# One input of a two-layer diffusion backbone loaded through another engine's queue, and one tile's low part made by another engine

## The chip, the cores and the metric

The kernel runs on one core of a Trainium2 chip. The metric is the time of one execution on the device, in microseconds. Five engines with their own instruction streams share the work: TensorE (PE, matrix products; PEld are its weight loads), VectorE (DVE), ScalarE (ACT), GpSimd (POOL) and SyncE (SP). They meet only through semaphores. Sixteen DMA engines move data between the chip's DRAM and its on-chip memory; here SP and ACT issue the transfers, each in its own instruction stream. A transfer that stands between two computations of ACT is issued when ACT gets there, and what stands behind it waits for it to be issued.

## The reference, cut to what matters

```python
for i in range(2):
    h_lat = rms_norm(x_lat, norm_g[i]) * (1 + sc_l) + sh_l      # 1024 latent tokens, width 1024
    h_ctx = rms_norm(x_ctx, norm_g[i]) * (1 + sc_c) + sh_c      # 256 context tokens
    if i % 2 == 0:   # two groups of 8 heads: A global attention, B windowed attention with a sink
        q, k, v, gate = split(h @ w_in)
        y = concat(A(q, k, v) * silu(gate), B(q, k, v) * silu(gate)) @ w_out
    else:            # convolution module and neighbourhood attention
        y = concat(conv(h), D(h) * silu(gate)) @ w_out
    x_lat = x_lat + g_l * y_lat                                 # the layer's input is added again
    x_ctx = x_ctx + g_c * y_ctx
return rms_norm(x_lat, final_g)
```

All of it is single precision. The two lines that matter here are the attention's product with the values, softmax(q k) v, and the residual sum, which needs the layer's input x a second time, after the attention.

## The kernel before

**Numbers in two parts.** TensorE is given each single-precision matrix as a high part (a rounded copy, made by ACT, line 336) and a low part (the number minus its rounded copy, made by POOL or DVE, line 339). `split` does this; its last argument names the engine of the low part, `"g"` for GpSimd and `"v"` for VectorE. A product is then three matmuls (lines 374 to 376).

**The first attention.** `attn_gen` goes through 252 items in the first layer. An item is a tile of 128 keys by 512 columns (128 queries of four heads). For each item PE makes the scores `st` (lines 543 and 547), ACT the exponential `pf` (line 555) and its high part `ph` (line 336), and POOL the low part `pl` (line 339); three items later PE multiplies `ph`, `ph` and `pl` with the values into `ov` (lines 483, 484 and 485). Every twelfth item (`vshare`, here 12) has its low part made by DVE instead. The scores have two PSUM banks, so PE can be at most two items ahead of ACT's exponentials. When a block of 128 queries is done, DVE transposes the sums (line 493), multiplies with the gate (713), inverts (496), spreads (497) and scales (717); the result `y` goes to DRAM (`Od`, line 720) or, for the last quarter of the heads, is split in place into `hh` and `hl`, a part of the input of the output projection.

**Woven into it.** While the last quarter of the heads is attended, the output projection of the first layer for the other three quarters runs between the attention's items (`out0_part`, products `po`, lines 374 to 376): for each pair of output columns `load_w` fetches six pieces of the weights (`wr<-ev_wo`, line 385), and at the first pass `load_x1` fetches the layer's input for these columns into `x1`, in three pieces: 256 context tokens (256 KB) and twice 512 latent tokens (512 KB each). Four calls make twelve transfers and 5 MB. DVE adds the products to `x1` in place (line 1198). The last quarter's own projection (`final_proj`) follows with and after the end of the attention; then `norm_h` and `make_h1` make the second layer's input (lines 354, 365, 366, 368 and 336/339).

**Order.** The kernel is written as generators that are interleaved by `weave`; a scheduler then orders each engine's instructions by priority and by its own estimate of time, and each engine runs its list strictly in that order. Every transfer gets one of eight completion semaphores, taken in turn by all transfers of both queues, and is not issued before the transfer that used the same semaphore last has landed. So at most eight transfers are under way, and a queue waits at its head for the one eight places back.

Of the kernel before, what the change touches and what calls it, by code (L numbers as in the profile page):

```python
# [101 lines left out]
def tile_kernel(ctx: ExitStack, tc: tile.TileContext, a, out):  # L102
    nc = tc.nc
    VE, SC, GP, PE, SY = nc.vector, nc.scalar, nc.gpsimd, nc.tensor, nc.sync
# [9 lines left out]
    mk, mwp, hold, layer, spare = [0], [None], [0], [0], []  # L114
# [3 lines left out]
    def bank(tag, name):  # L118
        if tag == "pp" and solo[0] and not sums[0]:
            turn[0] += 1  # L120
            tag = ("pp", "mx")[turn[0] // 2 % 2]
        return ps.tile([P, 512], F32, tag=tag, name=name, bufs=BUFS[tag])
# [3 lines left out]
    def nm(s):  # L126
        uid[0] += 1
        return f"{s}_{uid[0]}"
# [205 lines left out]
    def split(src, hi, lo, heng="s", leng="g"):  # L334
        if heng == "s":
            cast[0] = SC.copy(hi, src)  # L336
        else:
            VE.tensor_copy(hi, src)
        i_ = (GP if leng == "g" else VE).tensor_tensor(lo, src, hi.bitcast(F32), op=ALU.subtract)  # L339
        cast[2 if leng == "g" else 1] = i_  # L340
# [104 lines left out]
    def cut(ap, q, n):  # L445
        if isinstance(q, tuple):
            return ap.rearrange("p (r c) -> p r c", c=32)[:, q[0] : q[0] + q[1], q[2] : q[2] + q[3]]
        return ap[:, q : q + n]

    def flat(ap, q, n):  # L450
        return ap[:, :n].rearrange("p (r c) -> p r c", c=q[3]) if isinstance(q, tuple) else ap[:, :n]
# [12 lines left out]
    def attn_gen(pool, groups, vshare, look, nexts=None):  # L464

        preps = [g.prep for g in groups]
        items = [(g, t) for g in groups for t in range(len(g.tiles))]
        pend = []
        cnt = [0]

        def flush():
            g, t, ph, pl = pend.pop(0)
            k, q0, n, _ = g.tiles[t]
            if t == 0:
                g.ov = bank("mx" if g is groups[-1] and not layer[0] else "ov", nm("ov"))
                if g.load_v is not None:
                    g.load_v()
            V, vo = g.v(k)
            vo *= VW
            last = t == len(g.tiles) - 1  # L480
            o, ph, pl = cut(g.ov, q0, n), flat(ph, q0, n), flat(pl, q0, n)
            m = P if t == 0 else VW - 64
            PE.matmul(o[0:m], V[:, vo + 64 : vo + 64 + m], ph, start=(t == 0), stop=False)  # L483
            PE.matmul(cut(g.ov[0:64], q0, n), V[:, vo : vo + 64], ph, start=False, stop=False)  # L484
            pvs.append(PE.matmul(o[0 : VW - 64], V[:, vo + 64 : vo + VW], pl, start=False, stop=(last and g.sink is None)))  # L485
            if last:
                if g.sink is not None:
                    PE.matmul(g.ov, g.skm(), g.QL[0:76, :], start=False, stop=True)
                r1 = pool.tile([P, 8, 32], F32, tag="r1", name=nm("r1"), bufs=1)
                r8 = pool.tile([P, 8], F32, tag="r8", name=nm("r8"), bufs=2)  # L490
                rb = pool.tile([P, 256], F32, tag="rb", name=nm("rb"), bufs=1)
                for e in range(2):
                    VE.transpose(r1[e * 64 : (e + 1) * 64].rearrange("p a b -> p (a b)")
                                 .rearrange("p (a q) -> p a q", a=2), g.den(g.ov[64:128, :], e))
                yu = g.pre(g.ov)
                VE.reciprocal(r8, r1[:, :, 0])
                VE.transpose(rb, r8[:, :, None].broadcast_to([P, 8, 32]))
                g.finish(yu, rb)
# [13 lines left out]
        def prepare(x, n):  # L512

            while n and work and work[0][0] <= x:
                if next(work[0][1], work) is work:
                    work.pop(0)
                else:
                    n -= 1
# [7 lines left out]
        for x, (g, t) in enumerate(items):  # L526
            if x + AHEAD < len(items):
                items[x + AHEAD][0].ahead(items[x + AHEAD][1])
            if t == 0:
                g.start()  # L530
                while any(p is g.prep for _, p in work):
                    prepare(len(items), 1)
                for k in g.ids:
                    next(preps[k])
                    work.append((x + LEAD[layer[0]], preps[k]))
            rate = g.rate * max(len(work), 1)
            k, q0, n, extra = g.tiles[t]
            KA, KB = g.k()
            st = bank("st", nm("st"))
            kp = g.kpos[k] if g.bias else k  # L540
            cs = slice(kp * P, (kp + 1) * P)
            sf = flat(st, q0, n)
            sts.append(PE.matmul(sf, KA[:, cs], cut(g.QH, q0, n), start=True, stop=False))  # L543
            if not g.bias:
                for lhs, rhs in extra():
                    PE.matmul(st[:, :n], lhs, rhs, start=False, stop=False)
            PE.matmul(sf, KB[0:68, cs], cut(g.QL[0:68], q0, n), start=False, stop=True)  # L547
            ph = pool.tile([P, 512], F32R, tag="ph", name=nm("ph"), bufs=look + 1)
            pl = pool.tile([P, 512], F32R, tag="pl", name=nm("pl"), bufs=look + 1)
            pf = pool.tile([P, 512], F32, tag="pf" if layer[0] else "ost", name=nm("pf"), bufs=PFB)  # L550
            if g.bias and extra is not None:
                VE.tensor_tensor(flat(pf, q0, n), sf, extra(), op=ALU.add)
                SC.activation(pf[:, :n], pf[:, :n], AF.Exp)
            else:
                SC.activation(pf[:, :n], st[:, :n], AF.Exp, scale=1.0 if g.bias else SCALE)  # L555
            cnt[0] += 1
            split(pf[:, :n], ph[:, :n], pl[:, :n], "s", "v" if cnt[0] % vshare == 0 else "g")
            pend.append((g, t, ph, pl))
            tailc[:] = cast
            if t == len(g.tiles) // 2:  # L560
                g.gate()
            if t == len(g.tiles) - 1:
                g.last()
            prepare(x, rate // 2)
            yield
            if len(pend) > look:
                flush()
            prepare(x, rate - rate // 2)
            yield
# [166 lines left out]
    with ExitStack() as p0x:  # L736
# [307 lines left out]
        for j in PIECES:  # L1044
            load_kv(ORDER[0], *PIECES[j])
        SY.dma_start(KBs[ORDER[0]][0:64, :].bitcast(F32), Kd[ORDER[0]][0:64])
        main = attn_gen(a0, [group0(u, qb) for u in ORDER for qb in QORD], VS0, LOOK0)
        for k in range(3):
            u = ORDER[k]
            unit[0] = k  # L1050
            n = NSTEP[u // 2] + (12 if k == 0 else 0)
# [110 lines left out]
    with tc.tile_pool(name="o0", bufs=1, reuse_waits="tile", side="right") as op_:  # L1162
# [4 lines left out]
        x1 = []  # L1167
# [13 lines left out]
        def load_x1(e2):  # L1181
            for c in range(3):
                t0, n = CHUNKS[c]
                es = slice(2 * e2, 2 * e2 + 2)
                SC.dma_start(x1[c][:, es], a["cT"][:, es] if c == 0 else a["xT"][:, es, t0 - 256 : t0 - 256 + n])

        WO = 8

# [12 lines left out]
        def out0_part(fs):  # L1201
            for e2 in range(4):
                w = load_w(op_, a["ev_wo"], e2 * 256, 256, 256, WO, dks=fs, rb=2)
                if fs == parts[0]:
                    load_x1(e2)
                for e in (2 * e2, 2 * e2 + 1):
                    for c in range(3):
                        yield from out0(fs, e, c, *w)
# [83 lines left out]
    with ExitStack():  # L1292
# [476 lines left out]
        def ends(evs):  # L1769
            for ev in evs:  # L1770
# [8 lines left out]
                else:  # L1779
                    yield from final_norm(k, bcs[k])  # L1780

        main = attn_gen(dpool, groups1, VSH, LOOK1, {11: [], 12: [13, 14], 13: [15]})
        weave(main, WV[0], d_proj(2), 31, False, True, LAG[0])
        weave(main, WV[1], d_proj(3), 31, False, True, LAG[1])
# [149 lines left out]
```

## Time and profile before

| | us |
|---|---|
| median of three runs | 1478.57 (1475.46 to 1480.4) |
| the profiled execution, its own time | 1479.93 |
| its span | 1477.8 |
| PE busy in the span | 1415.7 (96%) |
| DVE, POOL and ACT busy | 1059.0, 828.4 and 741.1 |

The span reaches from the first to the last instruction; 2.1 us of the execution's time lie outside it. The stage that the change touches lies between 600 and 880 us of the span, counted from its start. In views of the timeline a row gives the start and the duration in microseconds, the engine (SPq and ACTq are issues of transfers), the line, the operation, the tiles, and in square brackets the idle time before it and what ended it.

### The profile page before, as it was taken

Reading aid. Unit: us, or ns where it says so; the run is one execution under the profiler, and the core shown is the slowest. Engines: PE = TensorE matmul, PEld = TensorE weight load, DVE = VectorE, ACT = ScalarE, POOL = GpSimd, SP = SyncE. Lnnn points to the kernel's source line nnn. Section 1 sums busy time; section 2 is a strip of 40 time slices with the busy share of each in tenths; the row PEclk is TensorE's granted clock in tenths of the full one; section 3 lists DMA queues with packets and bytes.
Section 4 is the critical chain, followed back from the end, with each engine's and each line's share of the span. In section 5 each row is a group of like instructions: output and inputs, shape, how many; then the busy total and the mean of one; then the engine's idle time right before and its main releaser. Section 6 shows DMA issues by size and latency. Waiting matters only on the chain.

```text
span 1477.8 us, 22207 instructions
## 1 busy us (share of the span) xinstructions
PE 1415.7 (96%) x7078; PEld 1151.4 (78%) x7078; DVE 1059.0 (72%) x2109; ACT 741.1 (50%) x1540; POOL 828.4 (56%) x819
## 2 busy tenths in 40 slices
PE   7899999999999999999999989999999999999996
PEld 2798978887888777667877778888887888778775
DVE  4786577589857786758666786999837575477775
ACT  3631453645364674764444655443434354555563
POOL 3561462656566785875554776754543343555564
PEclk9999999999999999999999999999999999999998
DMA  9675145323631235363222231213595877788623
GB/s 349 215 225 158 47 139 159 99 68 121 186 104 54 73 95 182 111 212 90 72 69 61 93 101 57 86 59 87 162 315 190 232 237 229 230 284 267 209 80 121
DMA packets 185228, 219.05 MB, mean 148 GB/s; under 512 B 17548, under 2 KB 136536, under 8 KB 185112
## 3 DMA queue, kind: packets, MB, share of 16 engines
q1 hardware_dynamic: 174864, 199.77, 43.3%
q10 hardware_dynamic: 10248, 17.87, 3.8%
q8 instruction: 56, 0.92, 0.3%
q14 instruction: 60, 0.49, 0.1%
HBM read 155.45 MB, written 62.13 MB: 147 GB/s over the span
## 4 chain that ended last, share of the span: by engine, by line
PE 79%; DVE 8%; DMA 7%; issue 2%; ACT 2%; POOL 1%; SPq 1%; ACTq 0%; DVEq 0%; POOLq 0%
PE p L374 7%; PE p L375 7%; PE p L376 7%; PE ov L483 4%; PE ov L485 4%; PE st L543 4%; PE ov L484 4%; PE st L547 4%; PE po L374 4%; PE po L375 4%; PE po L376 4%; PE pq L374 3%; PE pq L376 3%; PE pq L375 3%; PE pg L374 2%; PE pg L375 2%
## 5 line engine op out<-in xcount | busy, mean ns | idle before, releaser
L339 POOL TENSOR_TENSOR pl<-pf,ph 128x512 fp32r<-128x512 f32 (+1 forms) x327 | 385.9, 1193 | 242.4 <-ACT ph L336 190.2
L339 POOL TENSOR_TENSOR wl<-wr,wh 128x256 fp32r<-128x256 f32 (+2 forms) x253 | 193.2, 782 | 125.0 <-ACT wh L336 85.9
L555 ACT ACTIVATE pf<-st 128x512 f32<-128x512 f32 x284 | 166.1, 597 | 155.7 <-PE st L547 132.0
L336 ACT CAST ph<-pf 128x512 fp32r<-128x512 f32 (+3 forms) x364 | 203.3, 572 | 17.7 <-PE ov L484 6.7
L374 PE MATMUL p<-hh,wh 128*128 128x512 f32 x448 | 177.7, 399 | 1.1 <-ACT wh L336 1.0
L375 PE MATMUL p<-hl,wh 128*128 128x512 f32 x448 | 178.1, 400 | 0.0
L376 PE MATMUL p<-hh,wl 128*128 128x512 f32 x448 | 173.9, 397 | 0.2 <-POOL wl L339 0.2
L336 ACT CAST wh<-wr 128x256 fp32r<-128x256 f32 (+2 forms) x260 | 101.3, 404 | 140.5 <-DMA wr<-in_od_d_dram 38.6
L483 PE MATMUL ov<-ph,Vt 128*97 128x512 f32 (+4 forms) x364 | 137.9, 379 | 8.0 <-ACT ph L336 3.3
L543 PE MATMUL st<-QH,KAt 128*128 128x512 f32 (+3 forms) x364 | 138.8, 383 | 5.4 <-ACT pf L555 5.0
L485 PE MATMUL ov<-pl,Vt 128*97 128x512 f32 (+3 forms) x364 | 138.4, 380 | 4.2 <-POOL pl L339 3.9
L484 PE MATMUL ov<-ph,Vt 128*64 128x512 f32 (+3 forms) x364 | 135.1, 371 | 0.0
L547 PE MATMUL st<-QL,KBt 68*128 68x512 f32 (+3 forms) x364 | 132.7, 374 | 1.2 <-DVE QL L441 1.2
L671 DVE TENSOR_REDUCE mp<-mx 128x1 f32<-128x512 f32 x128 | 86.4, 683 | 56.7 <-PE mx L670 55.9
L1309 DVE SCALAR_TENSOR_TENSOR cps<-U,taps,cps 128x512 f32<-128x512 f32 x184 | 124.1, 750 | 0.0
L374 PEld LDWEIGHTS p<-hh,wh 128*128 128x128 f32 x448 | 84.5, 189 | 21.2 <-ACT wh L336 1.7
L376 PEld LDWEIGHTS p<-hh,wl 128*128 128x128 f32 x448 | 84.2, 188 | 20.2 <-POOL wl L339 0.6
L375 PEld LDWEIGHTS p<-hl,wh 128*128 128x128 f32 x448 | 84.5, 189 | 18.8 <-issue 0.2
L374 PE MATMUL pq<-wh,hh 128*128 128x384 f32 x256 | 88.0, 344 | 1.1 <-ACT pc L936 1.1
L376 PE MATMUL pq<-wh,hl 128*128 128x384 f32 x256 | 87.4, 342 | 1.6 <-POOL hl L339 1.6
L375 PE MATMUL pq<-wl,hh 128*128 128x384 f32 x256 | 87.5, 342 | 0.0
L543 PEld LDWEIGHTS st<-QH,KAt 128*128 128x128 f32 x364 | 69.5, 191 | 22.0 <-ACT pf L555 9.8
(302 smaller groups left out, 3437.4 us busy)
## 6 DMA issues: line engine op xcount, KB each, us to landing
mw<-in_mod_w_dram SPq DMA_DIRECT2D x28, 512.0 KB, 6.0
Q<-qs SPq DMA_DIRECT2D x40, 256.0 KB, 2.8
QH<-Q SPq DMA_DIRECT2D x80, 128.0 KB, 2.8
bm<-in_d_bm_dram SPq DMA_DIRECT2D x16, 540.0 KB, 5.5
wr<-in_od_d_dram SPq DMA_DIRECT2D x64, 128.0 KB, 3.2
wr<-in_ev_qkv_dram SPq DMA_DIRECT2D x32, 192.0 KB, 4.5
QD<-spq SPq DMA_DIRECT2D x48, 128.0 KB, 2.5
KAt<-KD SPq DMA_DIRECT2D x8, 768.0 KB, 7.2
```

Of the source, the lines that this page charges most:

```text
L336: cast[0] = SC.copy(hi, src)
L339: i_ = (GP if leng == "g" else VE).tensor_tensor(lo, src, hi.bitcast(F32), op=ALU.subtract)
L374: PE.matmul(o, lh, rh, start=first, stop=False)
L375: PE.matmul(o, lh, rl, start=False, stop=False)
L376: done[0] = PE.matmul(o, ll, rh, start=False, stop=last)
L483: PE.matmul(o[0:m], V[:, vo + 64 : vo + 64 + m], ph, start=(t == 0), stop=False)
L484: PE.matmul(cut(g.ov[0:64], q0, n), V[:, vo : vo + 64], ph, start=False, stop=False)
L485: pvs.append(PE.matmul(o[0 : VW - 64], V[:, vo + 64 : vo + VW], pl, start=False, stop=(last and g.sink is None)))
L543: sts.append(PE.matmul(sf, KA[:, cs], cut(g.QH, q0, n), start=True, stop=False))
L547: PE.matmul(sf, KB[0:68, cs], cut(g.QL[0:68], q0, n), start=False, stop=True)
L555: SC.activation(pf[:, :n], st[:, :n], AF.Exp, scale=1.0 if g.bias else SCALE)
L1309: VE.scalar_tensor_tensor(pc, uc, w, pc, op0=ALU.mult, op1=ALU.add)
```

## The change

The loads of the first layer's input (`load_x1`) are issued by SP instead of ACT. And the low parts of the attention's last two items (x of 250 and 251, in the first layer only) are both made by DVE. The last one was DVE's already, since 252 is a multiple of 12, so one item changes its engine.

```diff
@@ attn_gen @@
             cnt[0] += 1
-            split(pf[:, :n], ph[:, :n], pl[:, :n], "s", "v" if cnt[0] % vshare == 0 else "g")
+            split(pf[:, :n], ph[:, :n], pl[:, :n], "s", "v" if cnt[0] % vshare == 0 or (not layer[0] and x >= len(items) - 2) else "g")
@@ load_x1 @@
                 es = slice(2 * e2, 2 * e2 + 2)
-                SC.dma_start(x1[c][:, es], a["cT"][:, es] if c == 0 else a["xT"][:, es, t0 - 256 : t0 - 256 + n])
+                SY.dma_start(x1[c][:, es], a["cT"][:, es] if c == 0 else a["xT"][:, es, t0 - 256 : t0 - 256 + n])
```

The scheduler orders the instructions anew. On every engine the lists are the same up to the first of these loads and again from shortly after the end of the attention; between them many instructions change places by a few positions. Three places follow, with the rows of before marked - and the new ones +. The numbers at the names tell buffers apart.

ACT, where the last of the loads stood among the exponentials (`st`, `pf`, `ph` are one item's scores, exponentials and their high part):

```order
-L1185 DMA x_1825_7287<-in_xT_dram 128x2x512
 L336 CAST ph_7120<-pf_7122 128x512
-L1185 DMA x_1832_7311<-in_xT_dram 128x2x512
-L1185 DMA x_1818_7263<-in_cT_dram 128x512
-L1185 DMA x_1825_7287<-in_xT_dram 128x2x512
-L1185 DMA x_1832_7311<-in_xT_dram 128x2x512
 L555 ACTIVATE pf_7151<-st_7146 128x512
+L336 CAST ph_7149<-pf_7151 128x512
 L555 ACTIVATE pf_7178<-st_7173 128x512
```

Four loads in a row, between the high part of one item and the exponential of the next, are gone from ACT; so are the eight before them.

SP, where the loads now stand (`wr` are weights of the output projection, `gt` a block's gate, `Od` a finished block, `QH` the queries of a block to come):

```order
+L1185 DMA x_1825_7287<-in_xT_dram 128x2x512
 L720 DMA Od<-y_7018 128x2x128
 L385 DMA wr_7362<-in_ev_wo_dram 128x256
+L1185 DMA x_1832_7311<-in_xT_dram 128x2x512
 L385 DMA wr_7368<-in_ev_wo_dram 128x256
+L1185 DMA x_1818_7263<-in_cT_dram 128x512
+L1185 DMA x_1825_7287<-in_xT_dram 128x2x512
+L1185 DMA x_1832_7311<-in_xT_dram 128x2x512
+L1185 DMA x_1818_7263<-in_cT_dram 128x512
+L1185 DMA x_1825_7287<-in_xT_dram 128x2x512
+L1185 DMA x_1832_7311<-in_xT_dram 128x2x512
 L645 DMA QH_7248<-Q_4_113 64x2x256 x2
```

Five of the twelve stand ahead of the weight piece `wr_7362` (two of them even ahead of the gate `gt_7448`), one stands between it and `wr_7368`, and six between that and the queries `QH_7248`, whose load was next on SP before.

DVE, at the end of the attention (`x` and `hl` belong to the second layer's input, `pl` to the attention's last items):

```order
 L354 SCALAR_TENSOR_TENSOR x_1825_7287<-x_1825_7287,gs_93,bc_9716 128x512 x8
 L366 SCALAR_TENSOR_TENSOR hl_9722<-x_1825_7287,modT_91,hh_9721 128x512 x4
+L339 TENSOR_TENSOR pl_9613<-pf_9614,ph_9612 128x512
 L339 TENSOR_TENSOR pl_9625<-pf_9626,ph_9624 128x512
 L366 SCALAR_TENSOR_TENSOR hl_9722<-x_1825_7287,modT_91,hh_9721 128x512 x2
```

The last item but one's low part, `pl_9613`, now stands on DVE, behind twelve operations of the second layer's input and ahead of `pl_9625`; on POOL it stood just ahead of two more parts of the same input.

## The prediction

> **What bounds the kernel now.** First the page: which engine is full, and where not.
>
> ```profile
> PE 1415.7 (96%) x7078; PEld 1151.4 (78%) x7078; DVE 1059.0 (72%) x2109; ACT 741.1 (50%) x1540; POOL 828.4 (56%) x819
> ```
>
> TensorE sets the time; the others matter where they make it stand. The change can thus win only PE's idle time in the stage it touches, so I cut that stage into windows (columns: length, busy time and count of PE, PEld, DVE, ACT, POOL, then PE's granted clock, the DMA engines' share and GB/s).
>
> ```profile
> 630.00:635.00 5.00, 4.33 (x20) 2.94 (x18) 2.02 (x3) 0.62 (x1) 1.28 (x1) 1.00 1.04 375
> 635.00:640.00 5.00, 3.24 (x14) 2.15 (x15) 0.74 (x2) 3.81 (x8) 2.22 (x2) 1.00 1.05 390
> 640.00:660.00 20.00, 19.89 (x93) 14.73 (x92) 13.33 (x20) 15.74 (x30) 20.00 (x18) 1.00 0.61 170
> 660.00:680.00 20.00, 20.00 (x99) 15.94 (x98) 17.78 (x27) 9.05 (x16) 11.55 (x9) 1.00 0.19 58
> 680.00:690.00 10.00, 8.95 (x45) 6.70 (x44) 9.84 (x15) 3.08 (x8) 5.08 (x4) 1.00 0.60 172
> 690.00:700.00 10.00, 9.76 (x48) 7.57 (x47) 7.14 (x13) 7.19 (x14) 7.90 (x8) 1.00 0.20 64
> 840.00:860.00 20.00, 15.87 (x80) 11.29 (x80) 15.05 (x27) 18.02 (x34) 16.48 (x13) 0.95 0.24 75
> ```
>
> There are two holes: around 635, where DMA is saturated and ACT nearly idle, and before 860, where the attention ends. In between PE is nearly full; from 680 to 700 it misses another 1.3 us. The timeline shows who made the first hole:
>
> ```profile
> 624.11 0.47 PE L483 MATMUL ov<-ph,Vt 128*128 128x512 f32 x1 [0.54 <-DVE y L713]
> 635.11 0.90 ACTq L1185 DMA_DIRECT2D x<-in_xT_dram  x2
> 636.11 1.09 ACT L555 ACTIVATE pf<-st 128x512 f32<-128x512 f32 x2 [5.29 <-issue]
> 636.76 0.50 PE L543 MATMUL st<-QH,KAt 128*128 128x512 f32 x1 [2.44 <-ACT pf L555]
> ```
>
> and the chain of waits says why ACT stood so long:
>
> ```profile
> 626.71 8.38 DMA Od<-y
> 635.11 0.38 ACTq L1185
> 636.11 0.61 ACT pf L555
> ```
>
> ACT's last two loads of the input needed the completion semaphore of the block result `Od`, which landed at 635.09. An exponential that had nothing to do with it stood behind them, so no score bank came free and PE waited 2.44 us.
>
> **The change: the loads leave ACT.** Twelve issues go from ACT to SP. ACT's first effect is earlier still: the scores `st_7097` now stand ahead of the value products `ov_7062`, in the 0.54 us that PE waits for DVE at 624. Now the price on PE of this stretch, from the first `ov_7062` product at 624.11 to the first of `ov_7396`, the next block, at 645.12:
>
> ```profile
> 624.42 0.40 PE L484 MATMUL ov<-ph,Vt 128*64 128x512 f32 x1
> 624.65 0.39 PE L485 MATMUL ov<-pl,Vt 128*97 128x512 f32 x1
> 645.12 0.47 PE L483 MATMUL ov<-ph,Vt 128*128 128x512 f32 x1
> ```
>
> Starts lie 0.23 us apart at 512 columns (624.42 to 624.65), half of that at 256. The list of before has 70 products of 512 columns, 12 of 256 and a small transpose here: 70 x 0.232 + 12 x 0.116 + 0.12 = 17.8 us of work in 21.0 us, so 3.2 us are lost. Without the ACT wait, 2.4 to 3.2 of these come back, plus up to 0.5 for the scores that fill the hole at 624. What an item costs the engines that feed PE, from the page's groups (total and mean in ns):
>
> ```profile
> L339 POOL TENSOR_TENSOR pl<-pf,ph 128x512 fp32r<-128x512 f32 (+1 forms) x327 | 385.9, 1193 | 242.4 <-ACT ph L336 190.2
> L555 ACT ACTIVATE pf<-st 128x512 f32<-128x512 f32 x284 | 166.1, 597 | 155.7 <-PE st L547 132.0
> L336 ACT CAST ph<-pf 128x512 fp32r<-128x512 f32 (+3 forms) x364 | 203.3, 572 | 17.7 <-PE ov L484 6.7
> ```
>
> I walked the new list with 0.6 + 0.6 us on ACT and 1.2 to 1.3 on POOL for an item, and found PE never waiting: nearly every low part is there 1 us and more ahead of its use. Only `ov_7396` waits some 0.3 us for DVE to read the old sums. That makes 3.4; I take **3.0**, for weights may be late.
>
> How late? Two landings of the same 128 KB, alone and in the crowd:
>
> ```profile
> L385 SPq DMA_DIRECT2D wr<-in_ev_wo_dram x2: 352/386/420, 617.6 to 618.0; - x2
> ...
> DMA to landing us min/median/max: 2.8/2.8/2.9
> ```
>
> ```profile
> L385 SPq DMA_DIRECT2D wr<-in_ev_wo_dram x1: 560/560/560, 627.2 to 627.2; - x1
> ...
> DMA to landing us min/median/max: 8.9/8.9/8.9
> ```
>
> In the new order the piece `wr_7362` is issued at about 627.2 again, behind `Od`, which waits for DVE. The first 768 KB of input no longer wait for ACT and move before 624, while the DMA engines are idle. Ahead of the piece then stand a gate, two 512 KB pieces, one of 256 KB and `Od`: 1.5 MB, or 1.7 MB with itself, 4.5 us at 375 GB/s; with 2 us for landing it is there near 632. ACT comes to its rounding at 632.2, PE to its first use at 635. With the 8.9 us of before it lands at 636.1: ACT then stands 3.9 us at the weights, the `ph` behind them comes 1.2 us late, and with the scores behind it 1.7 to 2.4 us of the gain go. So this part lies between 1.0 and 3.7. The queries `QH_7248` follow all twelve loads: 5.2 MB from 624.6 at 383 GB/s (mean of 375 and 390) land near 641; PE asks for them near 644. The gain travels on where PE is full. The hole at 690 ends a chain of DVE, a load of SP and the landing of weights:
>
> ```profile
> 664.31 0.75 DVE x L1198
> ...
> 685.87 0.37 SPq L247
> 686.29 3.24 DMA wr<-in_ev_wo_dram
> ```
>
> Its first row adds a product of PE's to the input, so the chain starts, and ends, as much sooner as PE does.
>
> A rule speaks against the move. The Trainium skill, "DMA: Bandwidth & Descriptors", Queues, rings and completion order, says that each DMA engine takes turns between the queues that have work; then weights and `Od` on SP would pass the bulk on ACT, and lose that by sharing a queue. The trace disagrees: with the bulk on the other queue they took 8.4 and 8.9 us, about what all bytes issued ahead of them need (for `Od` a gate, four pieces of 512 KB, one of 256 and itself, 2.6 MB: 7 us at 375 GB/s and 2 for landing). By the rule the lateness above would be new, 1.0; by the rows it was there already, 3.0.
>
> **The change: one low part moves to DVE.** The rows of the end:
>
> ```profile
> 855.26 2.73 DVE L366 SCALAR_TENSOR_TENSOR hl<-x,modT,hh 128x512 fp32r<-128x512 f32 x4
> 856.56 3.17 POOL L339 TENSOR_TENSOR pl<-pf,ph 128x512 fp32r<-128x512 f32 x1 [1.70 <-ACT ph L336]
> 857.91 0.68 DVE L339 TENSOR_TENSOR pl<-pf,ph 128x512 fp32r<-128x512 f32 x1
> 858.51 1.76 DVE L366 SCALAR_TENSOR_TENSOR hl<-x,modT,hh 128x512 fp32r<-128x512 f32 x1
> 859.78 0.74 PE L485 MATMUL ov<-pl,Vt 128*97 128x512 f32 x1 [2.53 <-POOL pl L339]
> 861.97 0.92 DVE L493 STREAM_TRANSPOSE r<-ov 64x256 f32<-64x256 f32 x2
> 866.44 0.85 DVE L339 TENSOR_TENSOR hl<-y,hh 128x256 fp32r<-128x256 f32 x1
> 867.68 0.40 PE L375 MATMUL po<-hl,wh 128*128 128x512 f32 x1
> ```
>
> POOL's `pl_9613` took 3.17 us and PE waited 2.53 for it. On DVE it starts when the four operations before it are done, at 857.9, and ends at 858.6: PE goes on 1.1 us sooner. But what is late next? PE then has 36 products of the context tokens, and after them needs `hl` of the last block, which DVE makes at the end of an unbroken row: ready at 867.29, used at 867.68. So only 0.4 us of any gain of PE gets through, unless DVE's row ends sooner. It gets 0.68 us longer by the moved operation; if the two `L366` behind it stay at 1.76, `hl` comes at 867.9: a loss of 0.2. If one of them falls back to the 0.7 of its neighbours, since POOL's long operation is gone, `hl` comes at 866.9 and PE wins 0.5; if both do, 865.9, and PE wins up to 1.1. I take **0.3**, between 0.2 lost and 1.1 won.
>
> The Trainium skill, "SBUF — State Buffer", Who interferes with whom, bears on this: a VectorE operation with two inputs in SBUF and a GpSimd one block each other for a whole operation, whoever starts first. The trace agrees (3.17 and 1.76 where the two meet, 0.7 for the same DVE operation where DVE was first). By it the first `L366` finds no GpSimd operation under way, and the part gives 0.5.
>
> The clock stays out of the sum, for the same reason:
>
> ```profile
> 858.00:859.00 1.00, 0.00 (x0) 0.00 (x0) 1.00 (x2) 1.00 (x3) 1.00 (x1) 0.50 0.00 0
> 864.00:865.00 1.00, 1.00 (x7) 1.00 (x7) 1.00 (x4) 0.42 (x1) 0.00 (x0) 0.65 0.09 16
> ```
>
> It was halved at 858 and, by the mean of 0.65 in the second row, until about 864.6. From 859.78, where PE goes on, that is 4.8 us at half speed. If the shorter wait spares PE this, its products end 2.4 us sooner and it waits for `hl` instead.
>
> **Sum.** The profiled execution took 1479.93 us, its span 1477.8 and 2.1 around it. 1479.93 - 3.0 - 0.3 = 1476.6; the runs' median lies 1.36 lower, so **1475.3**, 0.2% faster. About 0.3%, 4.4 us here, is what a measurement of this kernel tells from no change.
>
> **Rivals.**
> - *More comes back.* DVE's row at the end is freed as well (1.1), the first part gives 3.7, and the new order shortens the 1.3 us lost from 680 to 700, where a weight load stood on SP behind a load that waits for DVE (L247); in the new list it stands ahead of it, 0.4 us sooner. 1478.57 - 3.7 - 1.1 - 0.4 = **1473.4**. For it: POOL and DVE slow each other just there. Against: DVE is full from 855 to 866.
> - *The wait only changes its engine.* SP stands at its eight-places rule instead of ACT, weights land as late as before and ACT stands at the rounding: of 3.0 there remain 1.0, and the end gives -0.2: **1477.8**. For it: the 8.9 us. Against: the bulk starts 3 us sooner.
> - *The queries come too late*, the one on the slow side. `QH_7248` now stands behind 5.2 MB on its own queue. PE takes its list in order and stops at the product that needs it, near 644. It decides when the bytes move below 300 GB/s (5.2 MB by 642, 2 us before the landing is wanted). They can:
>
> ```profile
> 628.00:629.00 1.00, 1.00 (x7) 0.80 (x6) 0.30 (x2) 0.55 (x2) 0.89 (x2) 1.00 0.92 191
> 629.00:630.00 1.00, 1.00 (x7) 0.83 (x6) 0.69 (x1) 0.00 (x0) 0.92 (x1) 1.00 0.91 227
> ```
>
>   With 209 for half of the bytes the mean is 270, and the queries land 2 us late; with 209 for all, 7.7. Between them, 4.5; with the weights late too and 0.2 lost at the end, 1478.57 - 1.0 + 4.5 + 0.2 = **1482.3**. For it: these two rows. Against: 375 to 390 in the ten microseconds behind them.
> - *The change hardly does what it says*: of the two last items one was DVE's already, so only one moves; this is in the sum. That the loads would still hold ACT is excluded by the new list.
>
> **Chances.** Forecast 0.45, more comes back 0.25, the wait changes its engine 0.18, queries late 0.12. The new order of some 300 instructions on ACT and DVE adds a scatter of 2 us to each, and the runs of before differ by 5. The forecast's own range is 1473 to 1478; with the neighbours, 1470.5 to 1480.5. Faster by over 0.3% (below 1474.1): most of the second case and the forecast's lower edge, 0.27. Slower by over 0.3% (above 1483): a part of the last, 0.09. Between: 0.64.
>
> **What would show it.** Right: no `[... <-ACT pf L555]` of over 1 us at 630 to 640, POOL busy through it, the loads in the rows of SPq, the start of the next block near 641 to 642, and all that follows some 3 us earlier up to the end of the attention; `pl` twice on DVE with 0.7, and PE waiting for DVE's `hl` before its products with it. Wrong: ACT waiting for `wr` or PE for `QH` there; holes of PE elsewhere between 645 and 840; or an end at which PE passes without waiting for DVE.

## The result, and the profile after

| | before | changed |
|---|---|---|
| median, us (8 runs each) | 1477.57 (1473.99 to 1483.21) | 1470.27 (1466.75 to 1475.06) |
| ratio | 1 | 0.9948 (95% interval 0.9928 to 0.9969) |
| profiled execution, its span | 1479.93, 1477.8 | 1475.06, 1473.0 |

The change takes 7.3 us off, between 4.6 and 10.6 by the interval. The interval lies clear of no change, and the median lies just below the range of the prediction (1470.5 to 1480.5, most likely 1475.3). The direction was the likeliest case's; the size was more than twice the 3.3 us of its sum, and a gain of over 0.3% had been given a chance of 0.27.

First the windows of the changed kernel, over the same stretches as before (length, busy time and count of PE, PEld, DVE, ACT, POOL, PE's granted clock, DMA share, GB/s):

```profile
630.00:635.00 5.00, 5.00 (x25) 3.83 (x24) 1.39 (x2) 3.22 (x7) 4.19 (x5) 1.00 1.04 367
635.00:640.00 5.00, 5.00 (x26) 3.92 (x25) 2.46 (x4) 3.19 (x6) 3.41 (x4) 1.00 1.05 387
640.00:660.00 20.00, 19.71 (x90) 14.53 (x89) 12.24 (x20) 13.82 (x27) 18.67 (x15) 1.00 0.68 187
680.00:690.00 10.00, 9.69 (x52) 7.67 (x51) 9.69 (x19) 3.67 (x9) 6.06 (x7) 1.00 0.57 173
690.00:700.00 10.00, 10.00 (x48) 7.79 (x47) 5.47 (x9) 6.62 (x12) 5.65 (x6) 1.00 0.13 39
840.00:860.00 20.00, 16.72 (x86) 11.54 (x85) 16.86 (x33) 16.80 (x33) 14.99 (x13) 1.00 0.22 66
```

From 630 to 640 the DMA engines are as full as before (1.04 and 1.05, 367 and 387 GB/s), and PE is full too: the hole has gone although the crowd has not. PE's idle time between 680 and 700 fell from 1.3 to 0.3 us. Before 860 PE is still idle for 3.3 us, but its clock is 1.00.

SP's own queue, where the loads now stand, in the timeline of the changed kernel:

```profile
624.74 0.57 SPq L649 DMA_DIRECT2D gt<-G  x1
627.46 0.37 SPq L720 DMA_DIRECT2D Od<-y  x1
627.92 0.41 SPq L385 DMA_DIRECT2D wr<-in_ev_wo_dram  x1
633.03 0.96 SPq L1185 DMA_DIRECT2D x<-in_xT_dram  x2
634.80 1.24 SPq L645 DMA_DIRECT2D QH<-Q  x2
```

and what the weight pieces issued at 627.9 and 628.9 took to land, and who waited for them:

```profile
L385 SPq DMA_DIRECT2D wr<-in_ev_wo_dram x2: 412/424/436, 627.9 to 628.9; - x2
...
  ACT wh L336: 0.4, 1
...
DMA to landing us min/median/max: 5.4/5.8/6.2
```

The last two loads leave SP at 633.03; behind them stand the queries, which land 8.3 to 8.6 us after their issue and make nobody wait. ACT, which had stood for 5.29 us, now waits 0.4 us for a weight. The end of the attention, again in the timeline:

```profile
854.80 1.28 DVE L339 TENSOR_TENSOR pl<-pf,ph 128x512 fp32r<-128x512 f32 x2
855.53 0.47 PE L485 MATMUL ov<-pl,Vt 128*97 128x512 f32 x1 [0.61 <-DVE pl L339]
856.00 1.40 DVE L366 SCALAR_TENSOR_TENSOR hl<-x,modT,hh 128x512 fp32r<-128x512 f32 x2
857.13 2.65 POOL L339 TENSOR_TENSOR hl<-x,hh 128x512 fp32r<-128x512 f32 x2 [4.80 <-ACT hh L336]
861.89 0.42 DVE L339 TENSOR_TENSOR hl<-y,hh 128x256 fp32r<-128x256 f32 x1
862.37 0.49 PE L375 MATMUL po<-hl,wh 128*128 128x512 f32 x1
```

PE waits 0.61 us for a low part where it had waited 2.53, the two `L366` take 0.70 us each instead of 1.76, and the products with the last block's `hl` start at 862.37 instead of 867.68. `hl` itself takes DVE 0.42 us instead of 0.85.

**Two stretches to measure by.** In the tables below, *first part* is the time from the first value product of the block that begins at 608.89 (before; 609.63 changed) to that of the last block (843.59; 840.32). *End* is the time from there to DVE's first operation of line 1428 in the second layer (near 1062; PE is full from 880 to 1000, so what is won is still there). For the changed kernel against the first profile of before they say: 234.7 to 230.7 and 218.2 to 216.3, together 6.0 us. The expectations of the experiments count up to DVE's line 292 near 886 instead; that row changes its place in some of the kernels, so line 1428 is used for all. By line 292 the whole stage took 277.4, 278.3 and 279.8 us in before, 271.5 and 272.0 in the changed kernel, 275.1 and 274.7 with the loads alone, 273.7 with GpSimd kept busy, 278.5 with three loads moved and 280.3 with the low part alone. Outside the two stretches the thirteen profiled executions took between 1015 and 1027 us, and not in an order that follows the change: most of the scatter of the whole time lies there, and the first pair of profiles differs by 4.8 us in the span although it differs by 6.0 in the stretches.

### The profile page after: what moved, and what is told of

It is laid out like the page before. It is cut to its first block, busy times and chain, and to the rows that moved or that the text cites. A ratio compares the mean times of both kernels' runs of the same rounds, so it can differ in the third digit from the quotient of the medians.

```text
span 1473.0 us, 22211 instructions
## 1 busy us (share of the span) xinstructions
PE 1415.2 (96%) x7078; PEld 1151.4 (78%) x7078; DVE 1059.3 (72%) x2110; ACT 740.5 (50%) x1540; POOL 826.1 (56%) x818
## 4 chain that ended last, share of the span: by engine, by line
PE 76%; DMA 9%; DVE 8%; issue 2%; ACT 2%; POOL 1%; SPq 1%; DVEq 0%; ACTq 0%; POOLq 0%
PE p L374 7%; PE p L375 7%; PE p L376 7%; PE ov L483 4%; PE ov L485 4%; PE ov L484 4%; PE st L543 4%; PE st L547 4%; PE po L374 4%; PE po L375 3%; PE po L376 3%; PE pq L374 3%; PE pq L376 3%; PE pq L375 3%; PE pg L374 2%
## 5 line engine op out<-in xcount | busy, mean ns | idle before, releaser
L374 PEld LDWEIGHTS p<-hh,wh 128*128 128x128 f32 x448 | 84.5, 189 | 22.1 <-ACT wh L336 2.8
```

The source lines that it names most:

```text
L374: PE.matmul(o, lh, rh, start=first, stop=False)
```

## The experiments

Three questions: do the two parts add up; is the end long because GpSimd and VectorE slow each other, or because PE waits and its clock falls; and why does the timed gain (7.3 us) exceed the 3.3 us of the sum and the 6.0 that the one pair of profiles shows. Each ratio stands against runs of the kernel before on the same chip.

| kernel | ratio (95% interval) | first part, us | end, us | last block to its `hl` on PE, us |
|---|---|---|---|---|
| before, three profiles | 1 | 234.7, 234.8, 236.2 | 218.2, 219.0, 219.0 | 24.1, 24.8, 24.8 |
| changed, two profiles | 0.9948 (0.9928 to 0.9969), 0.9951 (0.9929 to 0.9973) | 230.7, 231.0 | 216.3, 216.5 | 22.1, 22.4 |
| loads alone, two profiles | 0.9940 (0.9922 to 0.9957) | 232.3, 231.9 | 218.2, 218.3 | 24.0, 24.0 |
| low part alone | 1.0008 (0.9991 to 1.0025) | 236.4 | 217.3 | 23.1 |
| three of twelve loads | 0.9988 (0.9970 to 1.0007) | 233.4 | 220.6 | 26.6 |
| changed, GpSimd kept busy | 0.9948 (0.9929 to 0.9966) | 230.8 | 218.7 | 24.1 |
| changed, three pieces later | 0.9978 (0.9959 to 0.9996) | 230.9 | 221.6 | 22.3 |
| changed, six pieces later | 0.9972 (0.9948 to 0.9997) | 230.3 | 219.5 | 20.2 |
| changed, four pieces later | 0.9953 (0.9936 to 0.9970) | 231.2 | 216.0 | 20.2 |

### The loads alone

```diff
-                SC.dma_start(x1[c][:, es], a["cT"]... if c == 0 else a["xT"]...)
+                SY.dma_start(x1[c][:, es], a["cT"]... if c == 0 else a["xT"]...)
```

> Only the loads change their queue; the last low parts are made as before. Measured in the trace from the first product of the first block of the last quarter (608.89 before, 609.63 after the change) to DVE's L292 of the second layer's input (886.33 and 881.11): 277.4 us before, 271.5 with both parts. If the two parts add up as their holes do (PE idle 624 to 700: 4.4 us before, 0.6 with both), this kernel takes about 3.8 us off: 273.6 in the stage, a ratio of 0.9974, no PE wait over 0.5 us between 620 and 700, and an end as before: POOL's low part near 3 us, PE's wait for it 2.5 us, the granted clock halved behind it. If instead the end became shorter because the new order of the list upstream gives DVE a better start, the stage is 271.5 to 272.5 here and the second part of the change is worth nothing.

The ratio was 0.9940, all that both parts together gave: 8.9 us (6.4 to 11.5), where 0.9974 had been expected. PE's hole near 635 is gone and the first part takes 232.3 us, 2.4 less than in the first profile of before. The end is unchanged, 218.2, though GpSimd's low part took 1.75 us this time, not 3.17. DVE's `L366` behind it were slow again, 2.48 us for two. The timeline of this kernel:

```profile
640.62 0.72 PE L658 MATMUL mx<-KAt,QH 128*128 128x256 f32 x4 [0.42 <-DMA QH<-Q]
...
651.74 0.50 PE L543 MATMUL st<-QH,KAt 128*128 128x512 f32 x1 [1.14 <-ACT pf L555]
...
851.03 1.75 POOL L339 TENSOR_TENSOR pl<-pf,ph 128x512 fp32r<-128x512 f32 x1 [1.92 <-ACT ph L336]
853.25 2.48 DVE L366 SCALAR_TENSOR_TENSOR hl<-x,modT,hh 128x512 fp32r<-128x512 f32 x2
861.12 0.51 PE L375 MATMUL po<-hl,wh 128*128 128x512 f32 x1 [0.25 <-DVE hl L339]
```

The first row is the rival of the late queries: behind the twelve loads they took 10.0 us to land here, and PE waited 0.42 us for them. It happens, at a tenth of the price that the rival asked. The first part of this kernel is 0.9 to 1.6 us longer than that of the changed kernel, whose lists are the same up to the end of the attention. The second row shows where some of this lies: in both profiles of this kernel PE waits 1.14 us for an exponential there (no wait of over 0.5 us had been expected), and in the six profiles with both parts of the change at most 0.62 us at the same place. What delays ACT there was not followed. Of the 8.9 us that the time shows, the two profiles have 3.6 (3.1 in the first part, 0.5 in the end, means against before).

### The low part alone

```diff
-            split(pf[:, :n], ph[:, :n], pl[:, :n], "s", "v" if cnt[0] % vshare == 0 else "g")
+            split(pf[:, :n], ph[:, :n], pl[:, :n], "s", "v" if cnt[0] % vshare == 0 or (not layer[0] and x >= len(items) - 2) else "g")
```

> Only the low part of the last item but one goes to DVE; the loads stay on ACT. If the parts add up: the ACT wait of 5.3 us and the PE hole of 2.4 us near 635 stay as before, the end is 2.2 us shorter (stage 275.2 us against 277.4), L366 behind the low parts takes 0.7 us instead of 1.76, PE's clock stays at 1.00: ratio 0.9985. By the prediction's own price the end gives 0.3: stage 277.1, ratio 0.9998. If the end is shorter only thanks to the queue, the stage is 277.4.

The ratio was 1.0008. The end took 217.3 us, 1.0 to 1.8 less than in before, so the low part does shorten it without the queue. That is less than the 2.2 us expected, and only one of the two `L366` behind the low parts fell back (2.43 us for both); the granted clock fell to 0.50 in this end too, from 856.9 to 860.3, where 1.00 had been expected. But the first part took 236.4. The hole near 635 was there (this execution is some 3 us ahead by then), 2.56 us long, and this time the granted clock fell behind it. First the timeline's rows of the hole and of the two `L366`, then the windows behind the hole:

```profile
633.87 0.50 PE L543 MATMUL st<-QH,KAt 128*128 128x512 f32 x1 [2.56 <-ACT pf L555]
...
857.67 2.43 DVE L366 SCALAR_TENSOR_TENSOR hl<-x,modT,hh 128x512 fp32r<-128x512 f32 x2
```

```profile
636.00:637.00 1.00, 1.00 (x5) 0.81 (x5) 0.63 (x1) 0.93 (x3) 1.00 (x2) 0.50 1.05 393
637.00:638.00 1.00, 1.00 (x4) 0.71 (x3) 0.65 (x2) 0.82 (x2) 1.00 (x2) 0.50 1.05 284
638.00:639.00 1.00, 1.00 (x5) 0.71 (x4) 0.73 (x2) 0.00 (x0) 1.00 (x2) 0.77 1.11 234
```

The block from the first product at 620.92 to the next block took 22.7 us instead of 21.0. At this place nothing of that kind was in the profile on which the prediction rests. Is it this kernel's order, or chance?

### The kernel before, twice more

> The kernel before once more, for a second profile of the stage. In the kernel with only the low part moved, PE's hole near 635 was 2.56 us and TensorE's granted clock was 0.50 for about 3.4 us behind it (1.7 us lost); in the first profile of before the hole was 2.44 us and the clock stayed 1.00. Theory: a hole of this length is followed by the halved clock in some executions and not in others, so the one profiled execution understated what the hole costs. Then about every second profile of before shows a clock near 0.5 between 635 and 642, and its first block (from the first product of one block to that of the next) takes 22.7 us there and 21.0 otherwise. Rival: the halved clock belongs to the other kernel's own order; then this profile shows 1.00 there and 21.0 us.

> The kernel before a third time, with the same two theories as for the second profile: a first block of 22.7 us with a clock near 0.5 behind the hole in some of the profiles, or 21.0 us and 1.00 in all.

No edit. In the second profile the hole was 2.34 us, the clock 1.00 and the block 21.0 us. In the third it was 2.44 us, to the hundredth what the first had shown, and yet the clock fell and the block took 22.6 us. The third profile's row in the timeline, and its windows:

```profile
633.29 0.50 PE L543 MATMUL st<-QH,KAt 128*128 128x512 f32 x1 [2.44 <-ACT pf L555]
```

```profile
634.00:635.00 1.00, 1.00 (x4) 0.76 (x4) 0.00 (x0) 1.00 (x4) 0.70 (x1) 0.50 1.02 365
635.00:636.00 1.00, 1.00 (x4) 0.70 (x3) 0.00 (x0) 0.94 (x3) 1.00 (x2) 0.50 1.01 379
636.00:637.00 1.00, 1.00 (x5) 0.82 (x4) 0.68 (x2) 1.00 (x3) 1.00 (x2) 0.50 1.04 390
637.00:638.00 1.00, 1.00 (x6) 0.74 (x5) 1.00 (x3) 0.23 (x1) 1.00 (x2) 0.93 1.10 333
```

The microseconds behind the hole in the first profile, where PE comes back at 636.76:

```profile
636.00:638.00 2.00, 1.24 (x5) 0.81 (x6) 0.00 (x0) 1.89 (x4) 0.22 (x1) 1.00 1.06 388
638.00:640.00 2.00, 2.00 (x10) 1.33 (x9) 0.69 (x1) 1.92 (x5) 2.00 (x2) 1.00 1.04 385
```

So the same hole costs 2.4 us in one execution and 4.0 in another. The clock came down in two of the four profiles that have this hole at 2.3 to 2.6 us. The runs at large point the same way, but weakly: each lists its span and its mean granted clock, and the span times what the clock lacks of 1 is the time at half speed, halved. On one chip this is 21.1 us in the mean of 26 runs of before and 17.1 with the loads alone; on another it is 20.0 over 23 runs of before and 18.2 over ten of the changed kernel. It adds up all places of the program, the end of the attention too, and half speed at which PE had no work, so it does not show where the difference lies.

The Trainium skill, "TensorE: Matmul & The Clock Gate", What's actually happening, says that the clock is judged in a window of about 3.4 us that runs freely, so the moment depends on where in the window the work falls. The traces agree with both: the stretches at half speed behind this hole are 3.4 us long (at the end of the attention, in the three profiles of before, 6.8, twice that), and the same hole gets one or none. The same page of the Trainium skill, Why this matters for your kernels, allows gaps of up to some 3 us; here 2.44 us was enough in one execution of two.

### Three of the twelve loads

```diff
-                SC.dma_start(x1[c][:, es], ...)
+                (SY if e2 == 3 else SC).dma_start(x1[c][:, es], ...)
```

> Only the last three of the twelve loads (the pieces of the last pair of output columns) go to SP; nine stay on ACT, the end is as before. If what counts is that ACT does not stand at the head of the queue for the completion of the block result, moving the last three is nearly enough: ACT's longest wait for an issue near 630 is at most 2 us, PE's hole of 2.4 us goes, and the stage is 273.8 to 275 us (before 277.4, all twelve moved about 273.6). If what counts is that the bulk starts some 3 us earlier on SP and all goes in one order on one queue, the nine on ACT hold it as before and the stage is 276.5 or more.

The block result is no longer what ACT stands behind, yet it stands 4.62 us. The chain of waits of this kernel:

```profile
622.38 8.91 DMA x<-in_xT_dram
631.30 0.42 ACTq L1185
631.83 0.61 ACT pf L555
```

ACT's ninth load now waits for an earlier piece of the same input, eight places back, which took 8.91 us to land. PE's hole is 1.58 us instead of 2.44, and the block takes 18.6 us. The first part won 1.3 us against the first profile of before, of 4.0 with all twelve moved. The nine loads that are left hold ACT nearly as long, and the time shows no gain (0.9988): what has to leave ACT is thus not three loads but all that stand eight places behind a transfer in the crowd. The block result was only the one that happened to stand there. (Its end is 220.6 us, longer than in before, though nothing was changed there: GpSimd's last two low parts fell beside the first four `L366`, which took 4.79 us instead of the 2.73 of before.)

### GpSimd kept busy at the end

```diff
             split(pf[:, :n], ph[:, :n], pl[:, :n], "s", "v" if ... else "g")
+            (not layer[0] and x == len(items) - 2) and GP.tensor_tensor(pf[:, :n], pf[:, :n], ph[:, :n]..., op=ALU.subtract)
```

> Both parts of the change, and in addition GpSimd makes the last but one item's subtraction too, into a buffer that nobody reads again (it waits for DVE's own low part only because it writes in place). Nothing on PE depends on it: the program is the changed kernel plus one GpSimd instruction, every list else is the same. Theory 1 (the end was long because GpSimd and DVE slow each other): DVE's two L366 behind the low parts go from 0.70 to about 1.76 us again, hl of the last block comes 1.5 to 2.1 us later, PE waits for it, and the stage is 273 to 273.6 us instead of 271.5. Theory 2 (the end was long because PE waited 2.5 us for a late low part and then ran at half clock): PE gets its low part as early as in the changed kernel, the clock stays 1.00, and the stage is 271.5 to 271.9.

The timeline, and the window in which PE stood:

```profile
852.48 0.47 PE L485 MATMUL ov<-pl,Vt 128*97 128x512 f32 x1 [0.61 <-DVE pl L339]
852.57 1.61 POOL L557 TENSOR_TENSOR pf<-pf,ph 128x512 f32<-128x512 f32 x1 [3.28 <-DVE pl L339]
852.95 3.47 DVE L366 SCALAR_TENSOR_TENSOR hl<-x,modT,hh 128x512 fp32r<-128x512 f32 x2
858.38 0.36 PE L374 MATMUL po<-hc,wh 128*128 128x256 f32 x1 [2.63 <-DVE y L713]
```

```profile
856.00:858.00 2.00, 0.00 (x0) 0.00 (x0) 1.93 (x5) 0.00 (x0) 1.54 (x1) 1.00 0.00 0
```

This settles the second question. PE got its low part as early as in the changed kernel (0.61 us of waiting) and the clock stayed at 1.00; but with one GpSimd subtraction that nobody waits for, DVE's two `L366` took 3.47 us again, PE stood 2.63 us for DVE further on, and the end took 218.7 us instead of 216.3 and 216.5. In the profile the whole gain of the second part is gone; it came from DVE's row, not from PE's wait. The time does not show it: this kernel's ratio is 0.9948, as the changed kernel's.

### The changed kernel and the loads alone, again

> The changed kernel once more, for a second profile. If what the first one showed is the rule: PE never idle for over 0.6 us between the first product at about 609 and 700, clock 1.00 from there to the end of the attention, DVE's last two L366 at 0.70 us, and from the last block's first product to L292 40.8 us (before: 42.7, 43.5 and 43.6). If the end was a lucky sample, it takes 42 us or more here and the clock falls to 0.50 somewhere between 850 and 870.

> Only the loads moved, a second profile. If the low part that moves to DVE is worth about 2 us in the end of the attention, this kernel takes 42.5 to 43.6 us from the last block's first product to L292, with a stretch of half clock near 852, and the changed kernel 40.8; if the first pair of profiles was chance, the two overlap.

The ends are 216.5 and 218.3 us, next to 216.3 and 218.2 of the first profiles (by line 292, 41.0 and 42.8 us): by these profiles the second part of the change is worth 1.8 to 2.0 us. In the second profile of the changed kernel the clock did fall in the end,

```profile
854.00:856.00 2.00, 1.39 (x4) 0.82 (x4) 2.00 (x5) 2.00 (x4) 0.00 (x0) 0.66 0.00 0
856.00:858.00 2.00, 2.00 (x9) 1.76 (x9) 1.76 (x5) 0.85 (x2) 1.59 (x2) 0.50 0.03 10
```

and the end was only 0.2 us longer: PE's last value product came 0.19 us too late for DVE, and behind it DVE's row set the time, so half a clock cost next to nothing.

### Pieces of the second layer's input behind the last block

If DVE's row is the gate, its `L366` need not stand ahead of the last block's own work. Three kernels put some of the eight pieces (line 353 on, `dk`) behind the last block's `hl`: the last three, the last six, and the four with `dk` 2, 3, 5 and 6, whose low parts DVE makes. The bound was the last item's parts and is now the last block's. The edit of the kernel with six pieces (that with three has only its second half):

```diff
-            bound = tailc if l == 1 and c == 1 and dk >= 5 else [None] * 3
+            bound = tailc if l == 1 and c == 1 and dk >= 2 else [None] * 3
...
-        with tc.issue_after(sts[-4].ins):
-            run(nh[1])
+        with tc.issue_after(sts[-4].ins): tailc[:] = cast; run(nh[1])
```

> Both parts of the change, and the last three pieces of the second layer's input for these tokens (two L366 on DVE, their high parts on ACT, one low part on GpSimd) stand behind the last block's own hl instead of ahead of it. If DVE's row is the gate of the end, hl comes 1.4 us sooner and PE's products with it follow up to 0.9 us sooner, since its products of the context tokens end only then: from the last block's first product to L292 39.9 to 40.4 us instead of 40.8. If PE's own products are the gate, 40.8. The time itself cannot tell this (0.06%).

> As the kernel with the last three pieces moved, but with six of the eight behind the last block's hl, so that ACT makes the last high parts of the attention without the input's high parts in between and DVE reaches the last low parts 1.4 us sooner. Theory: DVE's row and ACT's are the gates; PE's idle time before the end of the attention (1.36 and 0.61 us) falls below 1 us and the end takes 38.5 to 40 us instead of 40.8. Rival: the pieces are then late for the convolution's first products (873 us in the changed kernel), PE waits there, and the end takes 40.8 to 42.

> Both parts of the change, and four of the eight pieces of the second layer's input (those whose low parts DVE makes, dk 2, 3, 5 and 6) stand behind the last block's own hl; the two that GpSimd makes stay where they were, since PE waited 2.2 us for them at 875 when they were moved too. Theory: PE gets to the products with the last hl 20.2 us after the last block's first product, as with six pieces moved (22.05 in the changed kernel), and nothing is given back at 875: to L292 39 us instead of 40.8, a ratio to before of 0.9935. Rival: the convolution's first products then wait for DVE's four pieces at 873 to 876, and the end takes 40.5 us or more.

With six or four pieces moved PE reaches the products with `hl` 20.2 us after the last block's first product, 1.9 to 2.2 sooner than in the changed kernel. Both rows moved at once, DVE's and ACT's: PE's two waits for the last high and low parts, 1.36 and 0.61 us in the changed kernel, shrank to one of 0.88 (six pieces) and 0.50 (four), so the two rows together were the gate, and how much is DVE's alone is not shown. With three pieces PE came to `hl` after 22.3 us, no sooner: here the clock fell during the last products of the attention, and DVE waited for PE. DVE's row and the window:

```profile
853.42 0.92 DVE L493 STREAM_TRANSPOSE r<-ov 64x256 f32<-64x256 f32 x2 [1.51 <-PE ov L485]
```

```profile
852.00:854.00 2.00, 2.00 (x8) 1.55 (x7) 0.57 (x2) 0.00 (x0) 1.04 (x1) 0.50 0.00 0
```

So half a clock is not always free at this place: the 1.4 us that DVE's row had won were lost in that wait. With three or six there is a loss further on, since GpSimd then makes its pieces behind the weights of the convolution, whose first products wait for them. With six, the waits of PE from 870 to 890:

```profile
PE p L375 <- POOL hl L339: 2.2, 1, 2.2
```

With three it was 1.7 us at 876.65, and two stretches at half clock behind it; the ends are 219.5 and 221.6 us. With four, that wait is gone and the end is 216.0, which is 0.3 to 0.5 us better than the changed kernel; of the 1.9 us the rest was lost between 870 and 1062, where this kernel's lists differ, and I did not follow it further. By line 292, the measure of the expectations, the last block took 43.6, 44.0 and 42.8 us with three, six and four pieces, more than the 40.8 of the changed kernel; there the moved pieces stand ahead of that row. The ratio of 0.9953 (0.9936 to 0.9970) cannot be told from the changed kernel's. No kernel here is shown to beat the changed one, and the changed one is not shown to beat the loads alone.

## Why the prediction was right or wrong

**Which step failed.** The mechanism was described rightly and both terms of the sum were too small. In the first pair of profiles the loads gave 4.0 us, not 3.0, and the low part 2.0, not 0.3; and the clock behind the hole near 635 stood in the sum at nothing, though it costs 1.6 us in some executions. The times put the failure elsewhere: the loads alone gained 8.9 us (6.4 to 11.5), and the low part alone nothing clear of noise (between 3.7 us lost and 1.3 won), so by them the term of 3.0 is the one that failed. The profiles of the loads alone show 3.6 us; where the rest of the 8.9 lies stays open.

**What bounds it** was read rightly: PE's holes at 635, 690 and before 860, in that order, and all three became smaller. That ACT stood for a completion that had nothing to do with it is borne out; that this was the block result's is true of before only, and the rule behind it (eight places back) is what counts, as the kernel with three loads moved shows.

**The loads, "I take 3.0", between 1.0 and 3.7.** The block that was walked by hand took 17.2 us instead of 21.0: 3.8, just above the upper bound. The walk had given 3.4; the 0.4 taken off for late weights was not needed. The first landed at 633.4, 5.4 us after its issue where 4.8 had been estimated; the two pieces cost ACT 0.4 us and PE nothing. They took 5.4 to 6.2 us to land on the shared queue against 8.9 with the bulk on the other one. By the rule quoted in the prediction (the Trainium skill, "DMA: Bandwidth & Descriptors", Queues, rings and completion order) the shared queue should have made them later. The trace has them sooner, but fewer bytes stood ahead of them this time, so this pair does not test the rule.

**"The clock stays out of the sum."** It was argued for the end of the attention, where it held nearly: behind the 0.61 us wait of the changed kernel the clock came down in one profile of two, and the end was 0.2 us longer. At the hole near 635 the clock was put at nothing, because the profile showed 1.00 there. That profile was one of two outcomes. In the other PE has work for all of the 3.4 us at half speed, and 1.6 us more are lost (22.6 against 21.0). The gain of removing this hole is then its length plus a chance of 1.6 us. From three profiles of before the first part is 235.2 us in the mean, against 234.7 in the one that the sum used.

**The low part, "I take 0.3, between 0.2 lost and 1.1 won".** The mechanism is the one described: DVE's row ends last, and two `L366` beside a GpSimd operation take 1.76 us each. The term was mis-sized: both fell back to 0.70, since GpSimd's next operation waits 4.80 us for ACT and starts at 857.13, when they are nearly done. The prediction had this case as "if both do", 1.4 us of DVE's row and 1.1 of PE's. The row became 1.7 us shorter (`hl` done at 862.31 instead of 867.29, from a start that was 3.27 us sooner), since `hl` itself, for which the sum kept 0.85 us, took 0.42; and PE's products with it, which had followed 0.39 us behind, now follow at once: 2.0 us. The upper bound was too low by these two pieces, and the value taken was the middle of three cases instead of the one that the rows of GpSimd pointed to. With the low part alone, one of the two fell back and PE came to `hl` 1.0 to 1.7 us sooner, where the prediction gave 0.5 for that case. One sign set down for a wrong prediction came too: PE goes into the products with `hl` at 862.37 without a wait. It had waited 0.56 us for DVE's `y` at 859.36 instead.

**The rivals.** *More comes back* is the case that the profiles show, with all three of its items: DVE's row, the first part at its upper end, and the hole at 690 (1.0 us, where 0.4 was set down). It gave 1473.4, and the median lies another 3.1 us below. *The wait changes its engine*: refuted, ACT waits 0.4 us. *The queries come too late*: they took 8.3 to 10.0 us to land and cost PE at most 0.4 us in any profile; 4.5 was the price set. *Hardly does what it says*: refuted.

**Where the 5.0 us between 1475.3 and 1470.27 lie.** The first part gave 4.0 us in the first pair of profiles, 1.0 more than taken; the end 2.0, which is 1.7 more; the other executions of before lose about 0.5 us more in the first part and 0.5 in the end than the profiled one (means of three: 235.2 and 218.8). The runs of before themselves had a median 1.0 us lower this time. That is 4.7. It is bookkeeping from profiles and not a proof: the rest of the program scatters by more from one execution to the next, and the times divide the gain in another way.

**What stays open.** The profiles say 4.4 us for the first part with both changes (235.2 against 230.9 in the mean; 3.1 with the loads alone) and 1.9 to 2.4 us for the end (means of the profiles). The times agree with the sum but not with the parts: loads alone gave 0.9940, more than its profiles show, the low part alone 1.0008, whose interval (down to 0.9991, 1.3 us) does not reach the 2 us, and GpSimd kept busy 0.9948, though its profile lost the 2 us again. The runs of one kernel differ by up to 14 us, so the times cannot divide 7 us between the two; that the second part shows in the time at all is not shown.

## What to carry to other kernels

A transfer that an engine issues between computations can make it stand for any transfer of the crowd, not for its own data; look at what stands at the head of such a queue, and give bulk loads to an engine that has nothing else to do. Price a hole of a full TensorE at its length and, where it is near 2.5 us as here, at a chance of some 1.6 us more for the clock, and take a second profile before trusting that the clock stays up. Time each part of a change by itself as well: a stage of a profile can show a gain that the times do not. Where two engines make the parts of one matrix by two-input operations, count the operation that slows the neighbour, not only the one that moves; here the row of the busier engine, DVE, set the end.

## What the runs showed of the hardware that was not expected

- The same hole of 2.44 us at the same place of the same program was followed by 3.4 us at a granted clock of 0.50 in one execution and by none in another.
- The same GpSimd subtraction, `pl` of the last item but one, took 3.17, 1.91 and 1.91 us in three profiles of the same kernel, and PE's wait for it 2.53, 1.28 and 1.29 us, with the same operations around it on DVE. The first profile had the longest, and in the other two the end was 0.8 us longer all the same: what GpSimd lost less, DVE lost more.
- Weights that share a queue with 5 MB of bulk landed sooner (5.4 to 6.2 us) than with the bulk on the other queue (8.9 us); how much of this is the smaller number of bytes ahead of them was not separated.
